# Storing two tiles through GpSimd's queue alone, and holding the first store back until ScalarE has done 54 copies

## The chip, the cores and the metric

The kernel runs on one core of a Trainium2 chip. The metric is the device time of one execution in microseconds. Five compute engines take part: TensorE (PE in the profile, with PEld for its weight loads), VectorE (DVE), ScalarE (ACT), GpSimd (POOL) and SyncE (SP, which only issues transfers). Transfers are carried out by 16 DMA engines, which serve all the queues of the core.

## The reference

```
batch, m, k, n = 16, 512, 1024, 768
x: (16, 512, 1024) float32    weight: (1024, 768) float32
scale: 0.1                    add_value: (16, 512, 768) float32
out = (scale * np.matmul(x, weight) + add_value).astype(np.float32)
```

The input and the output together are 87 MB, of which x is 33.6 MB and add_value and the output 25.2 MB each.

## The kernel before

**Tiles.** The 8192 rows of x are cut into 64 tiles of 128 rows. One partition of the on-chip memory holds 16 consecutive rows of a group of 2048, so a transfer of n neighbouring tiles is one contiguous run of n rows for each of the 128 partitions. The tile `xs` has 16 slots for x tiles; the tile `ao` has 32 slots, in which add_value is loaded, the result is written over it, and from which it is stored.

**Compute.** For four tiles at a time (a move) ScalarE and GpSimd each copy half of x, converted to bf16, into `va` in eight copies (line 167); VectorE transposes them (line 182); TensorE multiplies (line 214); VectorE scales the product and adds it to `ao`, two tiles at a time (line 191). The semaphores `by_act` and `by_pool` count the copies, `made` the finished tiles (from an offset `MADE`). So after n moves `by_act` stands at 8 n: 48 means that tiles 0 to 23 have been copied by ScalarE.

**Transfers.** SyncE issues nearly all transfers, in the order written out by hand in `STREAM`: each entry is an operation, a first tile and a number of tiles. "w" loads the weight, "x" loads x tiles, "a" loads add_value, "o" stores finished tiles, "a+" only makes up a semaphore count. SyncE works through the list strictly in order, and `need` makes it wait before an entry: an "x" waits until the slots that it overwrites have been copied by ScalarE and GpSimd; an "a" waits until the load before it has landed and until the store that frees its slots has landed; an "o" waits until its tiles are finished.

**The first stores.** Tiles 0 to 15 are stored in pieces: `("o", 0, 8)`, `("o", 9, 6)`, and apart from these tiles 8 and 15, the `PAIR`, as one strided access of two rows of 3 KB for each partition. The pair is split by partitions (line 31): SyncE stores the last 6 partitions (`BY_SP`, the entry `("pair", 8, 8)`), GpSimd's queue stores 5, 105 and 12 (`BY_POOL`), after its copies for the second round of x and before those for the third (lines 249 to 254). The load `("a", 40, 8)` reuses the pair's slots: it waits for the semaphores `pair_sem` and `aside_sem` (lines 123 to 125). The load `("a", 32, 8)` reuses the slots of tiles 0 to 7 and waits for their store.

**The end.** The last four tiles are stored by line 258, after all else.

Of the kernel before, what the change touches and what calls it, by code (L numbers as in the profile page):

```python
# [21 lines left out]
STREAM = [  # L22
# [5 lines left out]
]  # L28
FIRST, LAST = (0, 8), (60, 4)
PAIR, TURN_AT = slice(8, 16, 7), 2  # L30
BY_SP, BY_POOL = [(122, 6)], [(117, 5), (0, 105), (105, 12)]


@with_exitstack
def kernel(
# [8 lines left out]
    nc = tc.nc  # L44
# [14 lines left out]
    out_v = out_f.rearrange("(g p t) n -> p g t n", p=P, t=R)  # L59
    w_v = weight.rearrange("(c p r) n -> p c (r n)", p=P, r=2)  # L60

    def rows(view, s, n):
        assert s // R == (s + n - 1) // R
        return view[:, s // R, s % R:s % R + n, :]
# [5 lines left out]
    ao = const.tile([P, A_SLOTS, N], fp32, name="ao")  # L70
# [6 lines left out]
    x_sem = [tc.alloc_semaphore(f"x{i}") for i in range(X_SLOTS // MOVE)]  # L77
    a_sem = tc.alloc_semaphore("a")
    o_sem = [tc.alloc_semaphore(f"o{i}") for i in range(2)]
    pair_sem, aside_sem = (tc.alloc_semaphore(name) for name in ("pair", "aside"))  # L80
    by_act, by_pool, pool_go, turned, casts, done, made = (
        tc.alloc_semaphore(name)
        for name in ("by_act", "by_pool", "pool_go", "turned", "casts", "done", "made"))
# [1 line left out]
    MADE = TURNED + 2 + MM_BUFS - 2  # L85
    W_AT = A_SLOTS - KJ

    def slot(t):
        return t % A_SLOTS

    def store_pair(eng, p, n, sem):
        assert PAIR.stop <= R and PAIR.stop <= A_SLOTS
        eng.dma_start(out_v[p:p + n, 0, PAIR, :], ao[p:p + n, PAIR, :]).then_inc(sem, 16)  # L93

    def sync_engine(eng):
        groups, stores, known = 0, [], {}

        def need(sem, value):
            if known.get(sem, 0) < value:
                eng.wait_ge(sem, value)  # L100
                known[sem] = value

        for at, (op, s, n) in enumerate(STREAM):
            if at == SYNC_AT:
                eng.addr_align(HALF_BLOCK, offset=PAST, max_nops=0)
            last = s + n - 1
            if op == "w":
                dst = ao[:, W_AT + s:W_AT + s + n, :].rearrange("p (c r) n -> p c (r n)", r=2)
                move, sem = eng.dma_start(dst, w_v[:, s // 2:(s + n) // 2, :]), w_sem[s // 4]
            elif op == "x":  # L110
                k = s % X_SLOTS
                if last >= X_SLOTS:
                    moved = 8 * (last + 1 - X_SLOTS) // MOVE
                    need(by_act, moved)
                    need(by_pool, moved)
                move = eng.dma_start(xs[:, k:k + n, :], rows(x_v, s, n))  # L116
                sem = x_sem[k // MOVE]
            elif op == "a":
                if groups:
                    need(a_sem, 16 * groups)  # L120
                if last == A_SLOTS - 1:
                    need(casts, KJ)
                if s <= PAIR.start + A_SLOTS <= last:
                    need(pair_sem, 16 * len(BY_SP))
                    need(aside_sem, 16 * len(BY_POOL))
                if s >= A_SLOTS:
                    i = next(j for j, (a, b) in enumerate(stores) if a <= last - 1 - A_SLOTS < a + b)
                    need(o_sem[i % 2], 16 * (i // 2 + 1))
                move = eng.dma_start(ao[:, slot(s):slot(s) + n, :], rows(add_v, s, n))  # L129
                sem = a_sem  # L130
                groups += 1
            elif op == "pair":
                need(made, MADE + last + 1)
                for p, n in BY_SP:
                    store_pair(eng, p, n, pair_sem)
                continue
            elif op == "a+":
                need(a_sem, 16 * groups)
                eng.sem_inc(a_sem, 16 * (n // G - 1))
                groups += n // G - 1  # L140
                continue
            else:
                i = len(stores)
                if i > 1:
                    need(o_sem[i % 2], 16 * (i // 2))
                need(made, MADE + last + 1)
                move = eng.dma_start(rows(out_v, s, n), ao[:, slot(s):slot(s) + n, :])
                sem = o_sem[i % 2]
                stores.append((s, n))
            move.then_inc(sem, 16)  # L150
            if op == "x" and n == 2 * MOVE:
                eng.sem_inc(x_sem[k // MOVE + 1], 16)

    def mover(eng, copy, parity, count, go=None, first=0, turns=T // X_SLOTS):
        if go is None:
            eng.preload_act_table(mybir.ActivationFunctionType.Copy)  # L156
        with eng.Fori(16 * (first + 1), 16 * (first + turns) + 1, 16) as i:
            for q in range(X_SLOTS // MOVE):
                eng.wait_ge(x_sem[q], i)
                eng.wait_ge(turned, i + (4 * q - 12) if q < 3 else i)  # L160
                if go is not None:
                    eng.sem_inc(go, 1)  # L162
                k = MOVE * q
                src = xs[:, k:k + MOVE, :].rearrange("p i (c b k) -> p (i c) b k", b=4, k=64)
                for a in (parity, parity + 2):
                    for b in range(4):
                        copy(va[q % VA_BUFS][32 * b:32 * b + 32, :, a, :],  # L167
                             src[32 * a:32 * a + 32, :, b, :]).then_inc(count, 1)

    def vector_engine(eng):  # L170
        ao_g = ao.rearrange("p (g t) n -> p g t n", t=G)

        def cast_w(s, n):
            eng.wait_ge(w_sem[s // 4], 16)
            eng.tensor_copy(w_bf[:, s:s + n, :], ao[:, W_AT + s:W_AT + s + n, :]).then_inc(casts, n)  # L175

        def turn(move, half, moves=None):
            if half == 0:
                eng.wait_ge(by_act, moves)
                eng.wait_ge(by_pool, moves)  # L180
            q = 2 * half * KC
            eng.transpose(  # L182
                xt[:, 2 * half:2 * half + 2, :, :].rearrange("p i c m -> p (i c m)"),
                va[move % VA_BUFS][:, q:q + 2 * KC, :, :].bitcast(fp32).rearrange("p c a k -> p (c a k)"),
            ).then_inc(turned, 2)

        def finish(pair, at, products):
            eng.wait_ge(done, products)
            a = ao_g[:, at, 2 * pair:2 * pair + 2, :]
            q = 2 * (pair % 2)  # L190
            eng.scalar_tensor_tensor(  # L191
                a, mm[:, q:q + 2, 0:N], float(scale), a,
                op0=mybir.AluOpType.mult, op1=mybir.AluOpType.add).then_inc(made, 2)

        def group(i, at, last):
            eng.wait_ge(a_sem, i)
            for p in range(4):
                finish(p, at, i + (4 * p - 12) if p < 3 else i)
                if p < 2 or not last:
                    turn(1 if p < 2 else 0, p % 2, i + 8 if p == 2 else i)  # L200

        cast_w(0, 4)
        cast_w(4, 4)
        turn(0, 0, 8)
        turn(0, 1)
        with eng.Fori(16, 2 * T, 16) as i:
            group(i, bass.ds((i // 16 + A_SLOTS // G - 1) % (A_SLOTS // G), 1), False)
        s = slot(T - G) // G
        group(2 * T, slice(s, s + 1), True)
# [31 lines left out]
    s, n = FIRST  # L241
# [4 lines left out]
    with tc.tile_critical(no_gpsimd_drain=True):  # L246
        sync_engine(nc.sync)
        mover(nc.scalar, nc.scalar.copy, 0, by_act)
        mover(nc.gpsimd, nc.gpsimd.tensor_copy, 1, by_pool, pool_go, 0, TURN_AT)
        nc.gpsimd.wait_ge(made, MADE + PAIR.stop)  # L250
        for p, n in BY_POOL:
            store_pair(nc.gpsimd, p, n, aside_sem)
        nc.gpsimd.addr_align(HALF_BLOCK, offset=PAST, max_nops=0)
        mover(nc.gpsimd, nc.gpsimd.tensor_copy, 1, by_pool, pool_go, TURN_AT, T // X_SLOTS - TURN_AT)
        vector_engine(nc.vector)
        tensor_engine(nc.tensor)
    s, n = LAST
# [36 lines left out]
```

## Time and profile before

| | before |
|---|---|
| median of 3 runs | 208.54 us (208.38 to 208.83) |
| the profiled execution: its own time | 208.3 us |
| its span, first to last instruction | 206.5 us |
| TensorE's mean granted clock | 0.985 |
| moved by DMA | 87.04 MB, mean 422 GB/s |

A row of a timeline gives the start in us, the duration in us, the engine, the line of the kernel and the operation; x at the end is the number of instructions that were merged. A row of a DMA queue gives the number of packets, the megabytes and the time that the packets took, as a share of 16 engines times the window; a packet is counted, with its whole duration, in the window in which it starts, so in a short window a share can be far over 100%, and the mean duration of a packet is the share times 16 times the window, divided by the count. A row of DMA issues gives the number of issues, KB of each and the time from issue to landing. A row of stretches gives, for each window, the time, the busy time of PE, PEld, DVE, ACT and POOL with their instructions, the granted clock, the DMA share and GB/s.

### The profile page before, as it was taken

What the parts mean: (1) busy time and instruction counts of PE and PEld (TensorE: products, weight loads), DVE (VectorE), ACT (ScalarE), POOL (GpSimd) and SP (SyncE); (2) the same over time, 40 slices, a digit from 0 to 9 for tenths busy, and PEclk for the clock granted to TensorE, in tenths of its full rate; (3) what the DMA queues carried; (4) which work ended last, traced back from release to release, by engine and by line L of the source; (5) the groups of instructions that cost most, each with busy time, mean ns of one, the idle gap of its engine ahead of it and who ended that gap; (6) DMA issues with size and microseconds to landing.
All of it is one profiled execution on the core that took longest, in us unless ns stands there. A gap on an engine that the chain in (4) does not pass through costs nothing.

```text
span 206.5 us, 2224 instructions
## 1 busy us (share of the span) xinstructions
PE 167.6 (81%) x1008; PEld 50.4 (24%) x512; DVE 98.0 (47%) x66; ACT 134.7 (65%) x129; POOL 137.7 (67%) x135
## 2 busy tenths in 40 slices
PE   0000099999999999999999999999999997999900
PEld 0000023333322233333322333333222332333200
DVE  0004525537555555465555554655552854455320
ACT  2049980799999807999998069999990199910000
POOL 0049994699999906999999459999991199920000
PEclk9999999999999999999999999999999999999985
DMA  7989999999999999999999999999999999899995
GB/s 286 425 375 459 414 478 406 424 446 451 406 457 457 406 406 413 409 447 420 432 433 449 449 397 436 457 419 414 438 448 401 438 440 490 371 438 433 443 400 248
DMA packets 4067, 87.04 MB, mean 422 GB/s; under 512 B 476, under 2 KB 476, under 8 KB 1122
## 3 DMA queue, kind: packets, MB, share of 16 engines
q1 hardware_dynamic: 3874, 86.28, 97.7%
q0 software_dynamic: 192, 0.75, 0.9%
q14 instruction: 1, 0.01, 0.0%
HBM read 61.87 MB, written 25.17 MB: 421 GB/s over the span
## 4 chain that ended last, share of the span: by engine, by line
PE 46%; DMA 29%; POOL 9%; ACT 5%; issue 3%; DVE 3%; SPq 0%; DVEq 0%; POOLq 0%; ACTq 0%
PE mm L214 46%; DMA xs<-in_x_dram 15%; DMA out_dram<-ao 14%; POOL va L167 9%; ACT va L167 5%; DVE xt L182 2%; DVE ao L191 1%; SPq L129 0%; SPq L116 0%; DVEq L180 0%; DVEq L191 0%; SPq L100 0%; ACTq L160 0%; POOLq L162 0%; POOLq L160 0%
## 5 line engine op out<-in xcount | busy, mean ns | idle before, releaser
L214 PE MATMUL mm<-w_bf,xt 128*128 128x256 bf16 (+1 forms) x1008 | 167.6, 327 | 28.1 <-DVE xt L182 27.3
L167 POOL CAST va<-xs 32x1024 bf16<-32x1024 f32 x128 | 135.5, 1059 | 44.2 <-DMA xs<-in_x_dram 36.8
L167 ACT CAST va<-xs 32x1024 bf16<-32x1024 f32 x128 | 133.4, 1043 | 45.4 <-DMA xs<-in_x_dram 42.4
L191 DVE SCALAR_TENSOR_TENSOR ao<-mm,ao 128x1536 f32 (+1 forms) x32 | 56.2, 1757 | 73.2 <-PE mm L214 69.2
L212 PEld LDWEIGHTS <-xt 128*128 128x128 bf16 x512 | 50.4, 98 | 144.8 <-issue 116.7
L182 DVE STREAM_TRANSPOSE xt<-va 128x1024 f32<-128x1024 f32 x32 | 39.5, 1236 | 8.1 <-POOL va L167 6.0
L175 DVE CAST w_bf<-ao 128x3072 bf16<-128x3072 f32 x2 | 4.5, 2254 | 18.2 <-DMA ao<-in_weight_dram 18.2
L156 ACT ACT_TABLE_LOAD x1 | 1.3, 1283 | 1.3 <-SPq L246 1.3
L93 POOL DMA_DIRECT2D out_dram<-ao x3 | 2.0, 662 | 0.0
L275 POOL MEMSET const-float32-0.0<- 128x1 f32 x1 | 0.1, 98 | 0.2 <-issue 0.2
L275 POOL MEMSET const-bfloat16-1.0<- 128x1 bf16 x1 | 0.1, 101 | 0.0
L275 POOL MEMSET const-float32-1.0<- 128x1 f32 x1 | 0.1, 98 | 0.0
L275 POOL MEMSET const-uint8-127<- 128x1 uint8 x1 | 0.1, 98 | 0.0
## 6 DMA issues: line engine op xcount, KB each, us to landing
xs<-in_x_dram SPq DMA_DIRECT2D x7, 4096.0 KB, 21.6
ao<-in_add_value_dram SPq DMA_DIRECT2D x6, 3072.0 KB, 15.9
out_dram<-ao SPq DMA_DIRECT2D x3, 3072.0 KB, 28.5
ao<-in_add_value_dram SPq DMA_DIRECT2D x1, 6144.0 KB, 24.2
out_dram<-ao SPq DMA_DIRECT2D x1, 6144.0 KB, 31.2
out_dram<-ao SPq DMA_DIRECT2D x1, 4608.0 KB, 14.7
xs<-in_x_dram SPq DMA_DIRECT2D x2, 2048.0 KB, 21.0
ao<-in_weight_dram SPq DMA_DIRECT2D x2, 1536.0 KB, 17.0
```

The source lines that it names most:

```text
L93: eng.dma_start(out_v[p:p + n, 0, PAIR, :], ao[p:p + n, PAIR, :]).then_inc(sem, 16)
L156: eng.preload_act_table(mybir.ActivationFunctionType.Copy)
L167: copy(va[q % VA_BUFS][32 * b:32 * b + 32, :, a, :], src[32 * a:32 * a + 32, :, b, :]).then_inc(count, 1)
L175: eng.tensor_copy(w_bf[:, s:s + n, :], ao[:, W_AT + s:W_AT + s + n, :]).then_inc(casts, n)
L182: eng.transpose(xt[:, 2 * half:2 * half + 2, :, :].rearrange("p i c m -> p (i c m)"), va[move % VA_BUFS][:, q:q + 2 * KC, :, :].bitcast(fp ...
L191: eng.scalar_tensor_tensor(a, mm[:, q:q + 2, 0:N], float(scale), a, op0=mybir.AluOpType.mult, op1=mybir.AluOpType.add).then_inc(made, 2)
L212: eng.ldweights(x_j, tile_position=(0, 0))
L214: m = eng.add_instruction(mybir.InstMatmult(start_tensor_calc=(j == 0), stop_tensor_calc=(j == KJ - 1), tile_size=(P, P), tile_position=(0 ...
L275: nc = _bacc.Bacc("TRN2", target_bir_lowering=False, num_devices=1)
```

## The change

The entry "pair" and its semaphore go: SyncE no longer stores a part of tiles 8 and 15. GpSimd's queue stores all 128 partitions of them, in three stores of 6, 98 and 24 partitions. SyncE's store of tiles 0 to 7 has one wait more: until `by_act` has reached 54, which is six copies of ScalarE past the 48 that the x load ahead of it has waited for. Everything that follows in `STREAM` follows this store.

```diff
-    ("x", 32, 8), ("a+", 16, 16), ("o", 0, 8), ("o", 9, 6), ("pair", 8, 8), ("a", 32, 8), ("x", 40, 8),
+    ("x", 32, 8), ("a+", 16, 16), ("o", 0, 8), ("o", 9, 6), ("a", 32, 8), ("x", 40, 8),
...
+HOLD = {0: 54}
 PAIR, TURN_AT = slice(8, 16, 7), 2
-BY_SP, BY_POOL = [(122, 6)], [(117, 5), (0, 105), (105, 12)]
+BY_POOL = [(122, 6), (0, 98), (98, 24)]
...
-    def store_pair(eng, p, n, sem):
+    def store_pair(eng, p, n):
         assert PAIR.stop <= R and PAIR.stop <= A_SLOTS
-        eng.dma_start(out_v[p:p + n, 0, PAIR, :], ao[p:p + n, PAIR, :]).then_inc(sem, 16)
+        eng.dma_start(out_v[p:p + n, 0, PAIR, :], ao[p:p + n, PAIR, :]).then_inc(aside_sem, 16)
...
                 if s <= PAIR.start + A_SLOTS <= last:
-                    need(pair_sem, 16 * len(BY_SP))
                     need(aside_sem, 16 * len(BY_POOL))
...
-            elif op == "pair":
-                need(made, MADE + last + 1)
-                for p, n in BY_SP:
-                    store_pair(eng, p, n, pair_sem)
-                continue
...
                 need(made, MADE + last + 1)
+                if s in HOLD:
+                    need(by_act, HOLD[s])
                 move = eng.dma_start(rows(out_v, s, n), ao[:, slot(s):slot(s) + n, :])
```

More of the change, by code (lines that the diff above doesn't have):

```diff
@@ L79 @@
     o_sem = [tc.alloc_semaphore(f"o{i}") for i in range(2)]
-    pair_sem, aside_sem = (tc.alloc_semaphore(name) for name in ("pair", "aside"))
+    aside_sem = tc.alloc_semaphore("aside")
     by_act, by_pool, pool_go, turned, casts, done, made = (
@@ L251 @@
         for p, n in BY_POOL:
-            store_pair(nc.gpsimd, p, n, aside_sem)
+            store_pair(nc.gpsimd, p, n)
         nc.gpsimd.addr_align(HALF_BLOCK, offset=PAST, max_nops=0)
```

## The prediction

> **What bounds the kernel now.** I read the page first, for what is full.
>
> ```profile
> span 206.5 us, 2224 instructions
> DMA  7989999999999999999999999999999999899995
> q1 hardware_dynamic: 3874, 86.28, 97.7%
> q0 software_dynamic: 192, 0.75, 0.9%
> ```
>
> SyncE's queue (q1) keeps the 16 DMA engines occupied for 97.7% of the span, GpSimd's (q0) for 0.9%: together 98.6%, or 203.6 of 206.5 us. Only the first and the last slice of the DMA line are far from full. So this program is a list of transfers that run back to back, and its time is the sum of their packet times plus a ramp and a tail of about 2.9 us. The change moves the same bytes. It can shorten the run only by making packets shorter or by letting the last engine stop earlier, and lengthen it only by a hole in the queue or by loading the wrong engine.
>
> Next the timeline of SyncE's queue, where the edits are, and the landing times of what was issued between 72 and 74 us.
>
> ```profile
> 72.85 0.33 SPq L116 DMA_DIRECT2D xs<-in_x_dram  x1
> 73.36 0.82 SPq L147 DMA_DIRECT2D out_dram<-ao  x2
> 74.23 0.38 SPq L93 DMA_DIRECT2D out_dram<-ao  x1
> 95.96 0.36 SPq L129 DMA_DIRECT2D ao<-in_add_value_dram  x1
> 96.57 0.75 SPq L116 DMA_DIRECT2D xs<-in_x_dram  x1
> 114.98 0.33 SPq L129 DMA_DIRECT2D ao<-in_add_value_dram  x1
> 116.02 0.33 SPq L116 DMA_DIRECT2D xs<-in_x_dram  x1
> ```
>
> ```profile
> xs<-in_x_dram SPq DMA_DIRECT2D x1, 4096.0 KB, 15.7
> out_dram<-ao SPq DMA_DIRECT2D x1, 3072.0 KB, 22.5
> out_dram<-ao SPq DMA_DIRECT2D x1, 2304.0 KB, 28.1
> ```
>
> The load of x tiles 32 to 39 is issued at 72.85 and lands at 88.55; the store of tiles 0 to 7, issued at 73.36 right behind it, lands at 95.86; the store of tiles 9 to 14 at about 101.9. They land one after the other although all were issued by 74.2: a queue served in order, with 15 to 28 us of backlog. The store of tiles 0 to 7 cannot move a byte before the x load ahead of it is through.
>
> **The held store.** ScalarE's copies give the time of the new wait.
>
> ```profile
> 37.58 34.12 ACT L167 CAST va<-xs 32x1024 bf16<-32x1024 f32 x32 [7.48 <-DMA xs<-in_x_dram]
> 78.86 11.72 ACT L167 CAST va<-xs 32x1024 bf16<-32x1024 f32 x11 [7.16 <-DMA xs<-in_x_dram]
> ```
>
> Copies 17 to 48 end at 71.70, and copy 49 starts at 78.86, when the next x tiles have landed. One copy takes 11.72 / 11 = 1.065 us, so copy 54 ends at 78.86 + 6 x 1.065 = 85.25. SyncE therefore issues the store at about 85.3 in place of 73.36: 12 us later. Behind it on SyncE wait the store of tiles 9 to 14 (issued about 0.4 us after it) and the load at 95.96, which waits for the store's landing anyway. Nobody else waits for SyncE in that time, since the next x load needs POOL's copies, which end at 96.44 (POOL's row below). So the delay costs nothing if the descriptors arrive before the x load ahead runs out. When is that? I look at the last x packet of each engine before the store, and at the packet before it (windows 86.15 to 86.85 and 84.9 to 85.7 us, first two rows), then the same place before the second group of stores (134.7 to 135.62, third row), then the 1 us in which the 16 completions of the x load are written (87.3 to 88.3, fourth).
>
> ```profile
> q1 hardware_dynamic: 16, 0.52, 212.4%
> q1 hardware_dynamic: 16, 0.52, 152.3%
> q1 hardware_dynamic: 15, 0.49, 123.7%
> DMA packets 32, 0.39 MB, mean 393 GB/s; under 512 B 16, under 2 KB 16, under 8 KB 16
> ```
>
> A share is packet time over 16 engines times the window, so the mean packet took 2.124 x 16 x 0.7 / 16 = 1.487 us in the first window, 1.523 x 0.8 = 1.218 us in the second, 1.237 x 16 x 0.92 / 15 = 1.214 us in the third. The last x packet before the kernel's first store was 0.27 us too long on the mean engine; the one before the later stores was not. The 16 completions fall between 87.3 and 88.3. This is the one stall that I find inside the full stretch, and it sits exactly at the edit. Single engines suffer differently (windows of one packet, 86.18 to 86.22 and 86.51 to 86.525):
>
> ```profile
> q1 hardware_dynamic: 1, 0.03, 283.1%
> q1 hardware_dynamic: 1, 0.03, 525.0%
> ```
>
> 2.831 x 16 x 0.04 = 1.81 us and 5.25 x 16 x 0.015 = 1.26 us, so the excess is 0.05 to 0.60 us by engine. Without it the x load would end at 86.15 + 1.21 = 87.4 to 86.85 + 1.21 = 88.1. The held store, issued at 85.3, leads that by 2.1 to 2.8 us. Is that enough? Two kinds of rows bound it: the program's first load, and the two late stores at the end. Rows of the timeline, then the windows 1.7 to 2.0 and 2.0 to 2.7 with the first packets of that load, and 188 to 190:
>
> ```profile
> 0.74 0.38 SPq L243 DMA_DIRECT2D xs<-in_x_dram  x1
> 187.21 0.34 SPq L147 DMA_DIRECT2D out_dram<-ao  x1
> 197.87 0.33 SPq L258 DMA_DIRECT2D out_dram<-ao  x1
> ```
>
> ```profile
> q1 hardware_dynamic: 13, 0.43, 528.3%
> q1 hardware_dynamic: 3, 0.10, 38.3%
> ```
>
> ```profile
> 188.00:190.00 2.00, 2.00 (x14) 0.64 (x7) 0.34 (x1) 0.00 (x0) 0.00 (x0) 1.00 1.18 510
> ```
>
> The first load, issued at 0.74 into an empty queue, has 13 packets started between 1.7 and 2.0 and 3 more by 2.7: 1.0 to 2.0 us from issue to first packet. The store issued at 187.21 follows a transfer whose last packets end at about 190, and the engines show no hole (share 1.18, with packets counted where they start). So 2.0 us is enough for every engine by the first load, and 2.1 is what the earliest engine has. I expect no hole, by a thin margin of 0.1 us on the earliest engine and 0.8 us on the latest.
>
> What does the hold do to the 0.27 us? The trace of before shows no held store. From one side, if the stall comes from the store's descriptors lying in the queue behind the load, it goes: -0.27 us on the mean engine, -0.05 to -0.60 on the one that ends last. From the other, if it belongs to the first write to the output whenever that comes, it stays (0), and with little lead it grows: the first packets of the very first load took (5.283 x 0.3 + 0.383 x 0.7) x 16 / 16 = 1.85 us, 0.64 above the ordinary 1.214, so up to +0.37. I take -0.27. The stall is in the x packets, which are being read while the store's descriptors lie queued, and not in the store's own packets. The stores at 136 us show that a load followed by a store costs nothing in itself.
>
> **The pair of tiles.** These rows carry it: POOL's timeline, POOL's queue between 101 and 115 us, and one wave of it (103.45 to 104.2).
>
> ```profile
> 96.44 1.98 POOL L93 DMA_DIRECT2D out_dram<-ao  x3
> 98.47 17.48 POOL L167 CAST va<-xs 32x1024 bf16<-32x1024 f32 x16
> q0 software_dynamic: 192, 0.75, 13.0%
> q0 software_dynamic: 15, 0.09, 27.4%
> ```
>
> SyncE loses one issue (0.38 us at 74.23, while it had nothing else to do: 0). POOL issues three stores before and after, in 1.98 us; a store of 12 rows and one of 105 take 0.66 us each on average, so the new sizes cost POOL nothing and its copies still start at 98.47. The six rows that SyncE stored go to POOL's queue. A row costs an engine 0.130 x 16 x 14 / 122 = 0.239 us there, counting completions, so the total is the same.
>
> What changes is who carries the rows. A wave shows 15 row packets: 105 rows go as 7 on each of 15 engines, so one engine is spared. Fifteen is the largest number up to 16 that divides 105; by the same division 98 is 7 on each of 14, and 24 is 2 on each of 12. I take it that each store begins at the engine where the one before it stopped, and number the engines from the first store: before, the fifth has 1 + 1 of POOL's rows and the rest 8. After, the first four have 8, the fifth and sixth 3, the other ten 9. With SyncE's six rows on the first six, before is 9 on the first four and the sixth, 3 on the fifth, 8 on ten. So four engines lose a row (-0.24 us), ten gain one (+0.24), one loses six (-1.4) and the spared one stays. The Trainium skill states the division in "DMA: Bandwidth & Descriptors", section "Why a DMA increments its semaphore by 16 and not by 1": as many engines, up to 16, as divide the rows, the software queue going on from a cursor; the wave of 15 agrees.
>
> Which engine is last? These windows show the tail (204.1 to 205.3, then 202 to 204.1), a late packet of one engine beside four others of the same store (177.1 to 177.15, 179.0 to 179.1), and an instruction fetch (98.5 to 98.6).
>
> ```profile
> q1 hardware_dynamic: 24, 0.10, 19.9%
> q1 hardware_dynamic: 72, 0.88, 98.6%
> q1 hardware_dynamic: 1, 0.05, 233.4%
> q1 hardware_dynamic: 4, 0.20, 453.8%
> q14 instruction: 1, 0.01, 19.3%
> ```
>
> Until 204.1 all engines work; all end within the next 1.2 us. One engine is slow (2.334 x 16 x 0.05 = 1.867 us against 4.538 x 16 x 0.1 / 4 = 1.815), and another carries a fetch of 0.193 x 16 x 0.1 = 0.31 us. Nobody is far behind, so a row more or less on the last engine moves the end by -0.24 to +0.24. I take 0: the views do not name the last engine, and it is among ten of sixteen that gain or five that lose.
>
> Last, the landing of the pair gates the load issued at 114.98. Engines have two rows in the third store where they had one, and each further row waits for an x packet of 1.214 us in between: 1.45 us more, so issue at 116.4 at worst. That load's packets begin only when the x load issued at 96.57 is through. By its issue row
>
> ```profile
> xs<-in_x_dram SPq DMA_DIRECT2D x1, 4096.0 KB, 24.0
> ```
>
> it lands at 120.6 on its last engine, so at about 119.2 on its first, with the engines as far apart as in the tail: cover 2.8 us. The x load at 116.02 moves to about 116.9 behind it, covered by that load's own 7 us (3072 KB at the mean rate of 86.28 + 0.75 MB in 203.6 us). The price without cover would be the same 1.45 us.
>
> **Sum.** Held store -0.27, pair 0, SyncE and POOL 0: 208.30 - 0.27 = 208.03 for the profiled execution, whose span is 206.5 and which lies 0.24 below the median of the runs, 208.54. On the median: 208.27.
>
> ```profile
> PE mm L214 <- DVE xt L182: 1.1, 1, 1.1
> ```
>
> The saving reaches the end: TensorE waits for late x tiles once after 160 us (1.1 us), so it follows earlier loads, and the last store, issued at 197.87, has 2.6 us of queue before it.
>
> **Rivals.** 0.2% (0.42 us) is about what a measurement of this kernel can tell from no change.
>
> *The stall stays.* It belongs to the first store itself. The time is 208.54, with -0.24 to +0.24 for the rows. For it: every engine shows it at the same transfer, and only there. Against: it lies in the packet ahead.
>
> *A hole at the held store (slower).* If a store takes more than 2.1 us from issue to first packet on a busy queue, the earliest engines run dry; above 2.8 all do. At 3.5 us the hole is 3.5 - 2.45 = 1.05 us on the mean engine; with the stall of 0.27 gone that is +0.8: 209.3. The far bound is POOL's queue, whose first row packet started at 101.07 for an issue at 96.44, 4.6 us: +1.9, 210.4. For it: the margin is 0.1 us on the earliest engine, and the first load's latency was taken in an idle memory. Against: 2.0 us covers the slowest of 16 engines there, and the stores at 187 and 198 joined without a hole.
>
> ```profile
> q0 software_dynamic: 1, 0.01, 30.1%
> ```
>
> The row is POOL's queue in the window 101.05 to 101.1, with its first packet.
>
> *The slow engine is no longer spared.* If the new sizes are dealt out from the first engine upwards, the fifth has 1 + 7 + 2 rows in place of 3: +7 x 0.239 = 1.67 us on an engine that ends in the last 1.2 us: +0.5 to +1.7, about 209.6. The same section of the Trainium skill names such an exception for some of these stores, 100 rows lying on engines 0 to 14; no view here tells the two apart for 98.
>
> **Numbers.** Forecast (stall goes) 0.50, its own range 208.0 to 208.5, since with a row less on the last engine it is -0.51 and with a large share of the stall on that engine more: 0.26 of it lies below -0.42, 0.24 within. Stall stays 0.25, nearly all within (0.24). Hole 0.20: 0.18 slower, 0.02 within. Slow engine 0.05, slower. Faster 0.26, same 0.50, slower 0.24. The range runs from 207.9 to 208.9, which leaves out the larger holes and the slow engine.
>
> **What would show it.** Right: SyncE's store at 85.2 to 85.4 after 54 copies; last x packets before it of 1.21 us in place of 1.49; x load landing near 88.3; POOL's copies again at 98.5; the load of 114.98 at 115.5 to 116.5 with no hole after it; span about 206.2. Wrong: a dip of the DMA share at 87 to 89 us, x packets as long as before or longer there, or a tail after 204 in which one engine works alone.

## The result, and the profile after

| | before | after |
|---|---|---|
| median of six runs each | 208.5 us (208.38 to 208.83) | 209.5 us (208.99 to 210.07) |
| the profiled execution | 208.3 us, span 206.5 us | 208.99 us, span 207.2 us |

The ratio is 1.0048, with a 95% interval from 1.0037 to 1.0059: the changed kernel is slower by half a per cent. (A ratio comes from the single runs of both kernels, and need not be the quotient of the two medians.) The forecast was 208.27 us in a range of 207.9 to 208.9. The profiled execution is the fastest of its six; it shows 0.7 us of the 1.0 us.

The page after, with the rows that answer to those of before:

```profile
span 207.2 us, 2223 instructions
DMA  7989999999999999999999999999999999989995
q1 hardware_dynamic: 3856, 86.25, 97.4%
q0 software_dynamic: 208, 0.79, 0.9%
```

The DMA engines are as full as before, 98.3% of a span that is 0.7 us longer: 203.7 us in place of 203.6. The shares are rounded to 0.1% of the span, or 0.2 us; the sum of all packets of both queues in the two traces gives 203.73 and 203.48 us. So the packets take about 0.25 us longer on the mean engine, and the rest lies at the ends. SyncE's timeline after:

```profile
85.21 0.82 SPq L144 DMA_DIRECT2D out_dram<-ao  x2
95.73 0.34 SPq L129 DMA_DIRECT2D ao<-in_add_value_dram  x1
116.97 0.33 SPq L129 DMA_DIRECT2D ao<-in_add_value_dram  x1
198.04 0.33 SPq L255 DMA_DIRECT2D out_dram<-ao  x1
```

The first store is issued at 85.21 (forecast 85.3), the load behind it at 95.73, which is even 0.2 us earlier than before. The load that waits for the pair is issued at 116.97, 2 us later than before. Where the x load ends and the held store begins, the DMA share shows no hole (stretches of 1 us):

```profile
87.00:88.00 1.00, 1.00 (x8) 0.29 (x3) 0.68 (x2) 0.97 (x2) 0.94 (x2) 1.00 0.92 393
88.00:89.00 1.00, 0.95 (x7) 0.29 (x3) 0.95 (x1) 0.97 (x2) 0.94 (x2) 1.00 0.91 393
```

Now the packets. A row of SyncE's queue gives count, MB and share of a window, so share times 16 times the window, divided by the MB, is the packet time per MB. Ordinary packets take 37 to 38 us per MB, or 1.214 us for 32 KB and 0.686 us for the 18 KB of the store of tiles 9 to 14. First the changed kernel in three windows: 86.15 to 86.85 (the last x packets before the first store), 99.45 to 100.25 (the last store packets before the loads go on) and 133.5 to 135.95 (the last x packets before the second stores). Then the kernel before where the same transfers are, 99.75 to 100.45 and 133.5 to 135.95:

```profile
q1 hardware_dynamic: 16, 0.52, 174.1%
q1 hardware_dynamic: 18, 0.32, 128.3%
q1 hardware_dynamic: 33, 1.08, 111.4%
```

```profile
q1 hardware_dynamic: 16, 0.29, 98.6%
q1 hardware_dynamic: 33, 1.04, 98.4%
```

At 86 us the mean x packet takes 1.741 x 0.7 = 1.219 us: the stall of before (1.487 us) is gone. But the store packets at 99.5 us take 1.283 x 16 x 0.8 / 17 = 0.966 us (17 of the 18 carry data) against 0.986 x 0.7 = 0.690 us before, and the x packets at 134 us 40.4 us per MB against 37.1. So 0.27 us per engine is won at 86 us, 0.28 is lost at 99.5 us, and 3.3 us per MB x 1.08 MB / 16 = 0.22 at 134 us.

The rest is in the tail. The last store's issue row before and after, and the packets that start after 204.9 us before and after:

```profile
out_dram<-ao SPq DMA_DIRECT2D x1, 1536.0 KB, 7.7
```

```profile
out_dram<-ao SPq DMA_DIRECT2D x1, 1536.0 KB, 8.2
```

```profile
DMA packets 1, 0.00 MB, mean 0 GB/s; under 512 B 1, under 2 KB 1, under 8 KB 1
```

```profile
DMA packets 5, 0.01 MB, mean 11 GB/s; under 512 B 4, under 2 KB 4, under 8 KB 4
```

The last store is issued 0.17 us later and needs 0.5 us more until its last engine is through. After 204.9 us there was one completion left (a packet under 512 B, with which a transfer ends on each engine); now there are four, and an engine that still moves data alone. By the 16 last completions in each trace the mean engine ends at 204.88 in place of 204.55, 0.33 us later, and the last one at 205.80 in place of 205.16, 0.64 us later: it is 0.92 us behind the mean engine, where it was 0.61. The stalled packets differ from engine to engine (0.69 to 1.63 us for the last store packets at 99.5 us), which would leave the last engine further behind; which engine a packet belongs to no view shows, so for the tail this is argued and not shown.

### The profile page after: what moved, and what is told of

Same layout as the page of the kernel before. It is cut to its first block, busy times and chain, and to the rows that moved or that the text cites. A ratio compares the mean times of both kernels' runs of the same rounds, so it can differ in the third digit from the quotient of the medians.

```text
span 207.2 us, 2223 instructions
## 1 busy us (share of the span) xinstructions
PE 167.9 (81%) x1008; PEld 50.4 (24%) x512; DVE 98.0 (47%) x66; ACT 134.7 (65%) x129; POOL 137.4 (66%) x135
## 4 chain that ended last, share of the span: by engine, by line
DMA 38%; ACT 23%; PE 16%; POOL 9%; issue 6%; DVE 3%; ACTq 0%; DVEq 0%; POOLq 0%; SPq 0%
DMA xs<-in_x_dram 38%; ACT va L164 23%; PE mm L211 16%; POOL va L164 9%; DVE xt L179 2%; DVE ao L188 1%; ACTq L157 0%; ACTq L154 0%; DVEq L177 0%; POOLq L154 0%; DVEq L188 0%; POOLq L159 0%; POOLq L157 0%; DVEq L185 0%; SPq L101 0%
## 5 line engine op out<-in xcount | busy, mean ns | idle before, releaser
L164 POOL CAST va<-xs 32x1024 bf16<-32x1024 f32 x128 | 135.2, 1056 | 44.6 <-DMA xs<-in_x_dram 37.3
```

Source lines behind the costliest of these rows:

```text
L164: copy(va[q % VA_BUFS][32 * b:32 * b + 32, :, a, :], src[32 * a:32 * a + 32, :, b, :]).then_inc(count, 1)
```

## The experiments

Theories at the start: **A**, the hold costs, since it moves the stall to later transfers; **B**, the pair costs, by its rows or its spared engines; **C**, the stalls come from outside and stand elsewhere each time. Each kernel was timed against the kernel before on the same chip.

**Only the hold.** The kernel before, with these lines:

```diff
+HOLD = {0: 54}
...
+                if s in HOLD:
+                    need(by_act, HOLD[s])
```

> The kernel before, with the held store alone (54 copies); the pair is stored as before, six partitions by SyncE. Theory A (the hold costs): the hold moves the stall of the DMA engines from the x load at 86 us to later transfers, where it is larger, so the time is 209.2 to 209.6. Theory B (the pair costs: ten engines with a row more, the spared engine without its margin): the hold only takes the 0.27 us stall away, 208.1 to 208.4.

Measured: 209.81 us (before 208.44), ratio 1.0056 (1.0041 to 1.0072), 0.2 us above A's range. Windows 86.15 to 86.85, 99.45 to 100.2 and 133.2 to 136.1:

```profile
q1 hardware_dynamic: 16, 0.52, 174.1%
q1 hardware_dynamic: 18, 0.32, 118.4%
q1 hardware_dynamic: 33, 1.08, 105.2%
```

The same picture as in the changed kernel: no stall at 86 us, 0.84 us a store packet at 99.5 us, 45 us per MB at 134 us. The hold alone makes the whole loss. A holds, with a larger cost than it gave.

**Only the pair.** The changed kernel without the hold:

```diff
-HOLD = {0: 54}
+HOLD = {}
```

> The changed kernel without the hold: the pair in three stores of 6, 98 and 24 by GpSimd's queue, the store of tiles 0 to 7 issued as early as before. Theory A: 208.4 to 208.7, and the stall is back in the last x packets at 86 us. Theory B: 209.1 to 209.6, with the late engine of the tail (about 1 us behind the median engine) as in the changed kernel.

Measured: 208.19 us, ratio 0.9988 (0.9979 to 0.9996): faster than the kernel before, by 0.12%. Its window 86.15 to 86.85:

```profile
q1 hardware_dynamic: 16, 0.52, 218.4%
```

The stall is back at its place, 2.184 x 0.7 = 1.529 us a packet. B falls; the time is also 0.2 us below A's range, which allowed the pair no gain. This version beats both kernels, by little. Two kernels below that have the pair's change, and a hold that costs nothing, measure the same (0.9985 and 0.9984); what makes the gain is open.

**The changed kernel again.** No edit.

> The changed kernel once more, for a second profile. If the stalls at 99.5 to 101.5 and 133.5 to 137 us belong to the transfers there, they stand at the same places; if they come from outside (theory C), they stand elsewhere and their sum differs by tenths of a us. Time 209.3 to 209.7 by all theories.

Measured: 210.21 us, ratio 1.0079 (1.0064 to 1.0094), above the 209.7 that I gave. The stalls stand at the same places; windows 99.4 to 100.2, 102 to 108 and 135.2 to 136.9:

```profile
q1 hardware_dynamic: 17, 0.31, 125.1%
q1 hardware_dynamic: 85, 2.09, 87.0%
q1 hardware_dynamic: 17, 0.56, 90.5%
```

0.94 us a store packet, 1.45 us an x packet. Between 102 and 108 us the load packets take 0.870 x 16 x 6 / 2.09 = 40 us per MB, which the first profile of the changed kernel did not show. So the two places are the transfers' own (C falls for them), and the size at each varies from run to run; the slow stretch after 102 us is left open.

**An earlier hold.** The kernel before with `HOLD = {0: 50}`; the changed kernel with `{0: 52}` and with `{0: 53}`.

> The kernel before with the held store at 50 copies, 4.3 us earlier than 54 and about 7.6 us later than with no hold. Theory A in the form that a small lead matters (a queue that nearly runs dry): 208.4 to 208.7, like before. Theory A in the form that any hold moves the stalls: 209.2 or more. Theory B: 208.1 to 208.5.

> The changed kernel with the hold at 52 copies: SyncE issues the store of tiles 0 to 7 at about 83.1 us, some 4.5 us before the x load ahead runs out. Theory D (what costs is a queue that holds nothing behind its last transfer when that transfer's last packets start; the cost appears in later transfers): the stall stands in the last x packets at 86 us, none at 99 to 137, 208.1 to 208.4. Theory E (every hold costs in proportion to its length): 209.0 to 209.6.

> The changed kernel with the hold at 53 copies, one copy (1.07 us) earlier: SyncE issues the first store at 84.2 us; its descriptors reach the engines at about 85.2 to 86.2, just before the last x packets start. Theory D (queue dry when the last packets start) sets the border here: either the stall is back at 86 us and the time is 208.1 to 208.4, or it is not and the time is 209.2 to 209.8; something in between would mean that the engines differ.

Measured: 208.47 us, ratio 1.0002 (0.9989 to 1.0016), with 50 copies; 208.18 us, 0.9985 (0.9973 to 0.9996), with 52; 208.63 us, 1.0025 (1.0000 to 1.0050), with 53, where single runs reach from 208.21 to 210.77. SyncE's issue with 52 and 53, then the last x packets with 50 (86.2 to 86.65), 52 (86.3 to 86.85) and 53 (86.2 to 87):

```profile
83.16 0.82 SPq L144 DMA_DIRECT2D out_dram<-ao  x2
```

```profile
84.07 0.82 SPq L144 DMA_DIRECT2D out_dram<-ao  x2
```

```profile
q1 hardware_dynamic: 16, 0.52, 323.0%
```

```profile
q1 hardware_dynamic: 16, 0.52, 259.9%
```

```profile
q1 hardware_dynamic: 16, 0.52, 176.5%
```

3.230 x 0.45 = 1.45 us, 2.599 x 0.55 = 1.43 us and 1.765 x 0.8 = 1.41 us: with 50 to 53 copies the stall is where it was. The hold of 52 takes 10 us and costs nothing; one of 54 takes 12 us and costs 0.5%. The kernels with 52 and 54 differ in this one number alone. It is not the length that counts (E falls), and the border lies within one copy of 54. At 53 the median fell between the two ranges that D gave; the profiled execution (208.58) shows the stall at 86 us, and the slowest ones have no profile.

**A later hold.** `{0: 56}`.

> The changed kernel with the hold at 56 copies: the store is issued at about 87.4 us, when the x load ahead is ending. Theory D: a hole of about 1 us in the DMA share at 88 us and the later stalls too, 210.0 to 211.5. Theory E: 209.5 to 210.2, and no hole.

Measured: 211.27 us, ratio 1.0132 (1.0112 to 1.0151). SyncE's issue; two stretches of 1 us; the first store packets (88.25 to 88.5); the last packets of the second store (100.7 to 101.25). Time and hole are as D said:

```profile
87.44 0.82 SPq L144 DMA_DIRECT2D out_dram<-ao  x2
```

```profile
87.20:88.20 1.00, 1.00 (x8) 0.29 (x3) 1.00 (x2) 0.97 (x2) 0.94 (x2) 1.00 0.01 0
88.20:89.20 1.00, 0.95 (x7) 0.29 (x3) 0.85 (x1) 0.98 (x2) 0.94 (x2) 1.00 0.94 393
```

```profile
q1 hardware_dynamic: 16, 0.39, 374.7%
q1 hardware_dynamic: 16, 0.29, 246.7%
```

No packet starts in the first stretch (share 0.01): this is what a hole looks like. All 16 engines start the store between 88.25 and 88.5, 0.8 to 1.1 us after the issue. The later stall, at the turn from the stores back to the loads, is there too, and larger: 2.467 x 0.55 = 1.36 us a store packet in place of 0.69.

**The hold on the second store.** `{9: 54}` on the changed kernel: the same moment on SyncE, but with the first store queued.

> The pair as in the changed kernel, and the hold of 54 copies put on the second store (tiles 9 to 14) in place of the first: it is issued at the same 85.3 us, but with the 7 us of the first store queued ahead of it. Theory D: no cost, 208.1 to 208.4, stall at 86 us as before the change. Theory E, and any theory by which SyncE's late issue itself costs: 209.2 or more.

Measured: 208.23 us, ratio 0.9984 (0.9971 to 0.9996). No cost. The next-to-last (84.9 to 85.7) and the last x packets (86.15 to 87.1):

```profile
q1 hardware_dynamic: 16, 0.52, 182.8%
q1 hardware_dynamic: 16, 0.52, 140.7%
```

The stall is there, spread over two packets: 1.46 and 1.34 us in place of 1.214. D holds here, and what counts is thus not when SyncE issues, but whether a store lies behind the x load when that load's last packets start. An estimate from the latency above agrees: a store issued at 85.2 reaches the engines at 86.0 to 86.3, just when these packets start (86.15 to 86.85); one issued at 84.07 or 83.16 is there before them.

**The hold on a later store.** `{16: 93}` on the changed kernel, the first store early.

> The pair as in the changed kernel, the first store early, and the store of tiles 16 to 23 held until ScalarE has done 93 copies, about 134.6 us, some 2 us before the x load ahead of it runs out (in place of 117). Theory D: stalls in transfers after 137 us, above all where stores end and loads begin at 151 to 153 us, and 208.6 to 209.6. Theory F (only the kernel's first store matters, whatever the queue): 208.1 to 208.4.

Measured: 208.79 us, ratio 1.0011 (1.0001 to 1.0021), 0.23% above the pair alone. The profile does not explain it cleanly: at 85.0 to 85.7 us, 50 us ahead of the hold,

```profile
q1 hardware_dynamic: 16, 0.52, 271.1%
```

the first stall is 2.711 x 0.7 = 1.90 us a packet, the largest seen. After 137 us there is little to see. Windows 149.3 to 151 and 173.5 to 175.4, the next two turns:

```profile
q1 hardware_dynamic: 29, 0.71, 103.3%
q1 hardware_dynamic: 32, 0.79, 100.5%
```

That is 39.6 and 38.7 us per MB, where the kernel before has 37.2 and 37.3 (below). The time lies in D's range, and the stalls that D put after 137 us are hardly there, as by F. So the run decides for neither, and what costs the 0.23% stays open.

**Two holds.** `{0: 54, 16: 93}`.

> The changed kernel (54 copies) with a second hold: the store of tiles 16 to 23 waits for 93 copies, about 134.6 us, so that it too arrives when the x load ahead of it is at its last packets. Theory G (the first time that a load is followed by a store that is already queued, all engines stall; a hold only puts this off to the next such place): no stall at 133 to 137 us, but one at the next queued turn from loads to stores, the last add_value packets at 174 to 176 us; time 209.3 to 210. Theory H (the stalls come from how the engines lie against each other after the first hold): the stall at 133 to 137 stays.

Measured: 210.52 us, ratio 1.0112 (1.0095 to 1.0129), 0.5 us above G's range. Windows 133.5 to 136, 149.3 to 151 (the second stores' last packets) and 173.5 to 176.35 (the last load packets before the third stores); then the kernel before at 149.3 to 151 and 173.5 to 175.2:

```profile
q1 hardware_dynamic: 32, 1.05, 97.1%
q1 hardware_dynamic: 29, 0.71, 117.4%
q1 hardware_dynamic: 43, 1.06, 112.4%
```

```profile
q1 hardware_dynamic: 29, 0.64, 87.6%
q1 hardware_dynamic: 33, 0.81, 111.2%
```

37.0 us per MB at 134 us: that stall is gone. 45 us per MB at 150 us and 48 at 174 us, where the kernel before has 37.2 and 37.3: it has moved on to the next turns, and H falls. G said this ahead, for 134 and 174 us; the one at 150 us, a turn from stores to loads, it had not named.

**The load held too.** In the changed kernel, and in the one with two holds, the add_value load behind the first stores waits as well:

```diff
+HOLD, HOLD_A = {0: 54}, {32: 66}
...
+                if s in HOLD_A:
+                    need(by_act, HOLD_A[s])
```

> The changed kernel (54 copies) with the load of add_value tiles 32 to 39, which follows the first two stores, held until 66 copies (about 98.0 us in place of 95.7), so that it is not queued when the stores ahead start their last packets. Theory G, said of both directions: the stall at 99.5 to 102 us goes, the one at 133 to 137 stays, 209.0 to 209.4. If the load now comes too late: a hole at 101 us and 210 or more.

> All three holds together (54 copies, the load at 66, the second stores at 93). Theory G: only the stall at 174 to 176 us is left, 208.4 to 209.2. Theory H: stalls at other places, 209.5 or more.

Measured: 209.69 us, ratio 1.0071 (1.0054 to 1.0089), with the first hold, and 210.44 us, 1.0088 (1.0067 to 1.0109), with all three. In the first, SyncE's issue of the load; the last packets of the second store (99.5 to 100.19), both queues while the load behind it starts (100.46 to 101.3), and 132.8 to 136.3; then the kernel before while that load starts (100.45 to 101.35); then the second, 134.9 to 136.3, 149.3 to 151 and 173.5 to 176.9:

```profile
98.00 0.34 SPq L131 DMA_DIRECT2D ao<-in_add_value_dram  x1
```

```profile
q1 hardware_dynamic: 16, 0.29, 101.8%
q0 software_dynamic: 62, 0.22, 74.6%
q1 hardware_dynamic: 15, 0.17, 70.9%
q1 hardware_dynamic: 46, 1.43, 106.2%
```

```profile
q1 hardware_dynamic: 47, 0.38, 100.7%
q0 software_dynamic: 1, 0.01, 1.7%
```

```profile
q1 hardware_dynamic: 20, 0.57, 95.1%
q1 hardware_dynamic: 28, 0.69, 111.3%
q1 hardware_dynamic: 49, 1.20, 108.7%
```

With the first hold, the last store packets take 1.018 x 0.69 = 0.70 us: that stall is gone, as G said. But the first load packets take 0.709 x 16 x 0.84 / 0.17 = 56 us per MB, against 38 in the kernel before, and 134 us still has 42. GpSimd's queue has 62 packets in the same window, against one before, so how much of the 56 is theirs is not separated. The second kernel has 37, 44 and 49 in its three windows. Both times lie above G's ranges, the second in H's, but the stalls are where G has them, and at 150 us. So keeping the load back clears the last store packets and wins nothing. Whether that bears on G is open: by the latency above, as an estimate, a load issued at 98.00 is there at 98.8 to 99.1, ahead of the last store packets at 99.5, and so was queued after all. For the turn from loads to stores G held: in the four profiles with the first hold and the second store queued that are shown above, 134 us stalls; in the two with the first and the second store held, 134 us is clean and 174 us is not.

What the runs show together: where a load is followed for the first time by a store that is already queued, the mean engine loses 0.2 to 0.7 us, and the turns after it cost nothing (1.214 us a packet at 135 us, 37.2 and 37.3 us per MB at 150 and 174 us in the kernel before). If the store arrives only as the load's last packets start, this turn is clean, but the turn back to loads then stalls, and so does the next turn to a queued store. The hold does not remove a stall; it buys one turn and pays at two.

Why the engines need this once was not shown: nothing here looks inside an engine.

## Why the prediction was wrong, step by step

- **Time of the hold, and no hole.** Right: 85.21 us, and no gap in the packets. The bound for the latency, 2.0 us from the idle start, was twice what the 56-copy run shows (0.8 to 1.1 us), so the rival of a hole was given too much at 54 copies. At 56 the hole is real, about 0.6 of the 2.8 us: the last x packets, which start at 86.15 to 86.85, end at about 87.7 on the mean engine, and the store starts at 88.25 to 88.5.
- **"I take -0.27".** This is the step that failed: the term for the held store. The stall did leave 86 us (1.219 us a packet, as forecast), but I booked that as a saving. It came back at 99.5 us (+0.28) and at 134 us (+0.22), so the term is +0.2 in place of -0.27 on the mean engine of this profile, and more on the last; in time the hold alone costs 0.56%, about 1.2 us. My arguments, that the stall lay in the packets ahead and that the stores at 136 us turn without one, were both true and did not carry it: with the second store queued, the turn at 136 us is clean where the one at 86 us has stalled, and stalls where the one at 86 us is clean. The rival "the stall stays" had noticed that every engine shows it at the first store and only there, and priced it at 0; I had no rival in which it comes back later.
- **The tail.** I gave the last engine -0.24 to +0.24 for its rows and nothing for stalls of unequal size. It ends 0.92 us behind the mean engine in place of 0.61: an engine that works alone after 204 us was among the signs of being wrong. The pair's rows are not the cause: with the pair alone the last engine is 0.44 us behind, with the hold alone, and the old rows, 1.23. (The time from the last issue to its landing does not tell: 7.8 and 7.7 us in these two, against 8.2 in the changed kernel, because the last store is also issued later with the hold alone, at 199.16.) Over all profiles that distance is 0.42 to 0.92 us where the first stall stands before the first store, and 0.79 to 1.80 where it was moved; the two overlap, so what the hold added in one profile is not certain.
- **The pair.** 0 with -0.24 to +0.24; alone it measures -0.25 us (208.19 against 208.44), at the edge of that. The slow engine with more rows was to cost 0.5 to 1.7 us; nothing of it shows, so that rival falls.
- **The pair's landing.** Issue of the load behind it at 116.4 at worst; it was 116.97, and 116.14 with the pair alone. The pair alone is faster than before, so the cover held there; in the changed kernel SyncE's queue is at 99.1% between 116.5 and 118.8 us, so it held there too.
- **Range and chances.** 209.5 lies above 208.9. The slower side had 0.24, nearly all of it for two mechanisms, neither of which occurred. That the time did come out slower bears out nothing in the prediction.

## What to carry to other kernels

A stall that a profile shows once, at the first of several like places, may be a price that is paid once: before it is booked as a saving, ask what the later places would show without it. A transfer that is issued "just in time" can be late well before a hole is seen; here the border was, by estimate, about one packet (1.2 us) ahead of the end of the queue, and within one copy of ScalarE of the value chosen. Parts of an edit can have opposite signs: the pair alone is 0.12% faster, and the hold beside it costs about five times that.

## What the runs showed of the hardware

On a queue that was running empty (56 copies), the 16 engines started a store 0.8 to 1.1 us after its issue. The first turn from loads to an already queued store cost the mean engine 0.2 to 0.7 us (0.27 us in the kernel before, 0.32 with the pair alone, 0.68 with the later store held, in the last or next-to-last x packets); later turns cost nothing in the kernel before (37.2 and 37.3 us per MB). With the first store held, the turn back to loads cost 0.15 to 0.67 us in the last store packet (0.84 to 1.36 us in place of 0.69). With 53 copies, at the border, single runs of one kernel lie between 208.21 and 210.77 us.
